# Down projection as seven quarter-size products, with weight sums added up in DRAM

## The chip, the cores and the metric

The kernel runs on one core of a Trainium2 chip. The metric is the device time of one execution, in microseconds (us). The kernel before takes 2771.59 us, the median of three runs (2770.87 to 2773.34).

## What is computed

One layer of a hybrid decoder over 512 tokens of width 2048, in float32. The change touches the last product, `w_down` (5632 x 2048):

```
u = rmsnorm(h, norm1);  p = u @ w_in                  # 2048 x 10272
y = [SSD scan | RG-LRU | mLSTM](p)                    # three mixers, 4096 channels
h = h + y @ w_out
g, v = split(rmsnorm(h, norm2) @ w_gate_up)           # 2 x 5632 columns
h = h + (silu(g) * v) @ w_down                        # 5632 -> 2048
out = rmsnorm(h, norm_f)
```

## The kernel before

Every large product is made in float32 precision from three passes: each operand is split into a high and a low part (ScalarE writes the rounded high part, VectorE subtracts it), and TensorE computes high x high, high x low and low x high into the same PSUM bank. `halves` (lines 739 to 745) does this for a weight tile of 128x1024, `split_into` for an activation tile of 128x512, `three` (line 747) issues the three matmuls.

The program has these stages. First the input projection and the mixers: the columns of `w_in` are cut into 80 units of 128, in the order of `UNITS`; `unit` loads two halves of 128x1024 (`load`, line 126, on SyncE's queue, three buffers named raw), splits them and issues 48 matmuls (lines 147 to 149). The first half of units 0, 1 and 2 is loaded ahead. Each group of six units feeds one group of the SSD mixer: `conv` (line 255) needs a small memset of its tile `cin` by GpSimd (line 258), the scan's PE work is lines 336 to 393, and GpSimd multiplies the results (`y`, line 399 and before, and `gsq`, all recorded under line 87); TensorE sums `gsq` in `ps_g` (line 408). Then the output projection (`w_out`), then `seven` (lines 904 to 969) for each of 11 blocks of 512 gate and up columns. `seven` already multiplies quarter matrices by a scheme of seven products in place of eight; its weight sums are made in SBUF by accumulating DMAs that GpSimd issues (`more`, line 930, tile `k`). Its results go to DRAM as `at` (line 925).

The down projection of before is a plain product: `down` (line 994) makes the output in four blocks of 512 columns over two ranges of the inner dimension (6 and 5 blocks of 512), each weight tile serving two rows of 128 x four token tiles, 24 matmuls a tile. Activations come back from `at` as `ae` and are split. `finish` computes the last norm for two token tiles at a time.

The source order of the program isn't the order on the engines: the kernel is built with a list scheduler (`schedule_with_timeline_sim=True`), which places every instruction on its engine's in-order program by its own estimate of when its operands are ready. SyncE (SP) issues nearly all DMAs, GpSimd (POOL) the accumulating ones. Each of the two has eight completion semaphores in turn, so a DMA of a queue waits for the landing of the one eight before it.

Of the kernel before, what the change touches and what calls it, by code (L numbers as in the profile page):

```python
# [27 lines left out]
FB = 4  # L28
NB = NF // FB
NG = 8  # L30
EPS = 1e-6
BIG = 3.0e38
GELU_C = 0.7978845608028654
# [33 lines left out]
def trunk(tc, A, out):  # L67
# [663 lines left out]
    def acc_bank():  # L731
        return ps_ac.tile([P, T], F32, name="ac", tag="ac")

    def raw_tile(src):
        r = wpool.tile([P, 2 * T], F32, name="raw", tag="raw", bufs=3)
        sync.dma_start(out=r, in_=src)
        return r

    def halves(r):
# [147 lines left out]

    at_d = [dram.tile([4, P, T], F32, name=f"at{j}") for j in range(NB)]  # L890
    with tc.tile_pool(name="gu", bufs=2, reuse_waits="tile") as gu:
        def wk(src, tag):
            r = gu.tile([P, 2 * T], F32, name=tag, tag=tag, bufs=4)
            sync.dma_start(out=r, in_=src)
            return r

        def acts_in(j, make):

            for t in range(4):
                e = gu.tile([P, T], F32, name="ae", tag="e", bufs=3)  # L900
                sync.dma_start(out=e, in_=at_d[j][t])
                acts[j, t] = split_into(e, make)

        def seven(j, done=None):
            def src(quad, n):
                return A["w_gu"][j, quad, n]

            def save(ps, name):
                o = [gu.tile([P, T], F32, name=name, tag=name) for _ in range(2)]
                for a in range(2):  # L910
                    actf(o[a], ps[a], AF.Copy)
                return o

            def swiglu(t, g, u):
# [24 lines left out]
            more(s, 1)  # L939
            if not done:  # L940
                block(2, b3, lambda n: raw_tile(src(2, n)))
            for a in range(2):
                tt(dve, r1[a], r1[a], b3[a], ALU.add)
            if last:
                acts_in(0, etile)
            block(5, b2, lambda n: s[n])
            r5 = save(b2, "r5")
            v = [wk(src(3, n), "k2") for n in range(4)]
            more(s, 3)
            if last:  # L950
                acts_in(1, xtile)
            block(6, b1, lambda n: s[n], first=False)
            r2 = save(b1, "r2")
            if last:
                acts_in(2, xtile)
# [10 lines left out]
            if last:  # L966
                for i in (3, 4, 5):
                    acts_in(i, vtile)
            for a in range(2):
                swiglu(a + 2, b1[a], r5[a])  # L970

        acts = {}
        seven(0, (b1, b3))
        for j in range(1, NB):
            seven(j)


    with tc.tile_pool(name="dn", bufs=1, reuse_waits="tile") as dn:
        h = []
        for t in range(4):  # L980
            ht = dn.tile([P, KD * P], F32, name=f"hf{t}")
            sync.dma_start(out=ht, in_=h_d[t])
            h.append(ht)
        nf = dn.tile([P, KD * P], F32, name="nf")
        sync.dma_start(out=nf, in_=A["norm_f"].to_broadcast([P, KD * P]))
        fstats = const.tile([P, 4, 4, 6], F32, name="fstats")

        def act_of(js):
            def f(k, t):
                f = k % 4  # L990
                return tuple(v[:, f * P:(f + 1) * P] for v in acts[js[0] + k // 4, t])
            return f

        def down(js, mb, ts):

            cols = slice(mb * T, (mb + 1) * T)
            ps = token_rows([A["w_down"][mb, n] for n in range(2 * js[0], 2 * js[-1] + 2)], act_of(js), ts)
            for t in ts:
                tt(dve, h[t][:, cols], h[t][:, cols], ps[t], ALU.add)
                if js[-1] == NB - 1:  # L1000
                    dve.bn_stats(out=fstats[:, t, mb], in_=h[t][:, cols])  # L1001
                    if mb < 3:
                        tt(pool, h[t][:, cols], h[t][:, cols], nf[:, cols], ALU.mult)

        def finish(ts):
            for t in ts:
                cols = slice(3 * T, 4 * T)
                fmv = const.tile([P, 1, 2], F32, name=f"fmv{t}")
                dve.bn_aggr(out=fmv[:, 0], in_=fstats[:, t].rearrange("p a b -> p (a b)"))
                r = rms(fmv, 1, f"rf{t}")  # L1010
                tt(pool, h[t][:, cols], h[t][:, cols], nf[:, cols], ALU.mult)
                half_row = KD * P // 2
                actf(h[t][:, 0:half_row], h[t][:, 0:half_row], AF.Copy, scale=r)
                sync.dma_start(out=out[t][:, 0:half_row], in_=h[t][:, 0:half_row])
                dve.tensor_scalar(out=h[t][:, half_row:], in0=h[t][:, half_row:], scalar1=r, scalar2=None, op0=ALU.mult)
                sync.dma_start(out=out[t][:, half_row:], in_=h[t][:, half_row:])

        js = range(0, 6)
        for mb in range(4):
            down(js, mb, range(4))  # L1020
        js = range(6, NB)
        for j, make in zip(js, (vtile, etile, xtile, xtile, vtile)):
            for t in range(4):
                e = dn.tile([P, T], F32, name="ae", bufs=3)
                sync.dma_start(out=e, in_=at_d[j][t])
                acts[j, t] = split_into(e, make)
        for mb in range(3):
            down(js, mb, range(4))
        for ts in ((0, 1), (2, 3)):
            down(js, 3, ts)  # L1030
            finish(ts)
# [35 lines left out]
def pack(x, norm1_w, w_in, ssd_conv_w, ssd_conv_b, ssd_dt_bias, ssd_a_log, ssd_d, ssd_norm_w,  # L1067
# [12 lines left out]
    a["w_down"] = moving(w_down[0])  # L1080
# [44 lines left out]
```

## Time and profile before

| | |
|---|---|
| median of the runs | 2771.59 us |
| the profiled execution | 2771.48 us |
| its span, first to last instruction | 2769.6 us |
| PE busy | 2733.8 us, 99% |
| DVE, ACT, POOL busy | 56%, 40%, 11% |
| DMA, mean | 154 GB/s; HBM read 384.43 MB, written 32.61 MB |

The profile has a page with the busy time of each engine and the chain of work that ended last, and the trace answers queries: a timeline of one engine, busy times in stretches (windows), groups of instructions by line. A stretch is given in us from the span's start. PE is TensorE, DVE is VectorE, ACT is ScalarE, POOL is GpSimd, SP is SyncE. MB is 10^6 bytes; a tile of 128x1024 float32 is 0.524 MB.

### The profile page before, as it was taken

How to read it: one execution, taken by the hardware profiler on the slowest of the kernel's cores; microseconds unless marked ns; L12 is line 12 of the kernel's file. 1: busy time of each engine (PE TensorE's matmuls, PEld its weight loads, DVE VectorE, ACT ScalarE, POOL GpSimd, SP SyncE). 2: the span in 40 equal slices, each digit the busy share in tenths (PEclk: the TensorE clock that was granted, in tenths of full speed). 3: DMA queues.
4: the chain of work that ended last, by engine and by line, in shares of the span. 5: the costliest groups of instructions: out<-in, count | busy, mean ns of one | idle time of the engine just before them, and what ended most of it. 6: DMA issues, size and time to landing. Idle time of an engine off the chain costs nothing.

```text
span 2769.6 us, 32286 instructions
## 1 busy us (share of the span) xinstructions
PE 2733.8 (99%) x12566; PEld 2236.9 (81%) x12566; DVE 1547.0 (56%) x2035; ACT 1104.8 (40%) x1319; POOL 314.5 (11%) x337
## 2 busy tenths in 40 slices
PE   8999999999999999999999999999999999999998
PEld 5888888888778877888878888888888878888886
DVE  8766666666677786324465555555555563233335
ACT  5433333333355565212244444444444452122113
POOL 2111111111011110000011112111111110000001
PEclk9999999999999999999999999999999999999999
DMA  4433333323233255544488898899888875234225
GB/s 170 136 107 106 111 107 102 97 98 120 89 125 131 100 179 175 168 153 138 143 223 212 205 202 197 206 203 200 198 202 204 216 196 212 94 112 133 99 92 182
DMA packets 139769, 425.46 MB, mean 154 GB/s; under 512 B 17052, under 2 KB 19132, under 8 KB 138976
## 3 DMA queue, kind: packets, MB, share of 16 engines
q1 hardware_dynamic: 114272, 331.11, 35.8%
q0 software_dynamic: 25344, 92.29, 18.4%
q8 instruction: 98, 1.61, 0.2%
q14 instruction: 55, 0.45, 0.1%
HBM read 384.43 MB, written 32.61 MB: 151 GB/s over the span
## 4 chain that ended last, share of the span: by engine, by line
PE 97%; DMA 1%; DVE 1%; ACT 0%; issue 0%; ACTq 0%; SPq 0%; DVEq 0%
PE ac L749 20%; PE ac L750 20%; PE ac L751 20%; PE mm L147 11%; PE mm L149 11%; PE mm L148 11%; PE ps_d L388 1%; PE tp L922 1%; DMA ae<-at 1%; PE ps_l L450 1%; DMA k<-in_w_gu 0%; PE ps_i L634 0%; PE ps_st L362 0%; PE ps_o L393 0%; PE ps_c L643 0%; DVE wlo L87 0%
## 5 line engine op out<-in xcount | busy, mean ns | idle before, releaser
L750 PE MATMUL ac<-wlo,vh 128*128 128x512 f32 x2192 | 857.8, 391 | 2.1 <-DVE wlo L87 1.9
L751 PE MATMUL ac<-whi,vl 128*128 128x512 f32 x2192 | 855.1, 391 | 0.0
L749 PE MATMUL ac<-whi,vh 128*128 128x512 f32 x2192 | 807.7, 391 | 6.6 <-ACT whi L93 6.6
L87 DVE TENSOR_TENSOR wlo<-raw,whi 128x1024 fp32r<-128x1024 f32 x370 | 457.8, 1237 | 608.7 <-ACT whi L93 599.0
L93 ACT ACTIVATE whi<-raw 128x1024 fp32r<-128x1024 f32 x370 | 391.5, 1058 | 942.8 <-PE ac L751 545.0
L147 PE MATMUL mm<-uh,whi 128*128 128x512 f32 x1280 | 507.4, 396 | 1.8 <-DVE og L87 1.0
L149 PE MATMUL mm<-uh,wlo 128*128 128x512 f32 x1280 | 504.6, 394 | 0.0
L148 PE MATMUL mm<-ul,whi 128*128 128x512 f32 x1280 | 504.1, 394 | 0.0
L749 PEld LDWEIGHTS ac<-whi,vh 128*128 128x128 f32 x2192 | 412.4, 188 | 95.4 <-ACT whi L93 7.7
L750 PEld LDWEIGHTS ac<-wlo,vh 128*128 128x128 f32 x2192 | 412.8, 188 | 90.3 <-DVE wlo L87 4.9
L87 DVE TENSOR_TENSOR wlo<-k,whi 128x1024 fp32r<-128x1024 f32 x260 | 318.2, 1225 | 295.4 <-ACT whi L93 294.0
L751 PEld LDWEIGHTS ac<-whi,vl 128*128 128x128 f32 x2192 | 412.6, 188 | 84.9 <-issue 0.2
L93 ACT ACTIVATE whi<-k 128x1024 fp32r<-128x1024 f32 x260 | 275.2, 1060 | 337.1 <-PE ac L751 306.9
L147 PEld LDWEIGHTS mm<-uh,whi 128*128 128x128 f32 x1280 | 240.5, 188 | 60.6 <-issue 6.9
L149 PEld LDWEIGHTS mm<-uh,wlo 128*128 128x128 f32 x1280 | 240.4, 188 | 53.8 <-issue 4.2
L148 PEld LDWEIGHTS mm<-ul,whi 128*128 128x128 f32 x1280 | 240.7, 188 | 50.8 <-issue 3.0
L930 POOL DMA_DIRECT2D k<-in_w_gu x176 | 152.5, 869 | 1015.2 <-DVE wlo L87 668.0
L749 PE MATMUL ac<-whi,uh 128*128 128x512 f32 x256 | 99.9, 390 | 0.0
L750 PE MATMUL ac<-wlo,uh 128*128 128x512 f32 x256 | 99.9, 390 | 0.0
L751 PE MATMUL ac<-whi,ul 128*128 128x512 f32 x256 | 99.0, 389 | 0.0
L90 DVE SCALAR_TENSOR_TENSOR cacc<-cin,half,cacc 128x512 f32<-128x512 f32 x96 | 81.2, 846 | 1.2
L87 POOL TENSOR_TENSOR hf<-hf,nf 128x512 f32<-128x512 f32 x16 | 25.1, 1594 | 485.9 <-DVE fstats L1001 485.9
(269 smaller groups left out, 1881.2 us busy)
## 6 DMA issues: line engine op xcount, KB each, us to landing
k<-in_w_gu POOLq DMA_DIRECT2D x176, 512.0 KB, 5.6
raw<-in_w_in SPq DMA_DIRECT2D x160, 512.0 KB, 3.7
raw<-in_w_down SPq DMA_DIRECT2D x98, 512.0 KB, 3.3
k<-in_w_gu SPq DMA_DIRECT2D x88, 512.0 KB, 4.1
raw<-in_w_out SPq DMA_DIRECT2D x64, 512.0 KB, 3.5
raw<-in_w_gu SPq DMA_DIRECT2D x48, 512.0 KB, 19.9
at<-e SPq DMA_DIRECT2D x44, 256.0 KB, 3.7
ae<-at SPq DMA_DIRECT2D x44, 256.0 KB, 4.1
```

The lines of the kernel that those rows point to most:

```text
L87: eng.tensor_tensor(out=o, in0=a, in1=b, op=op)
L90: dve.scalar_tensor_tensor(out=o, in0=a, scalar=s, in1=b, op0=op0, op1=op1)
L93: act.activation(out=o, in_=a, func=f, **kw)
L147: pe.matmul(ps, lhsT=wh, rhs=xh[:, cols], start=k == 0, stop=False)
L148: pe.matmul(ps, lhsT=wh, rhs=xl[:, cols], start=False, stop=False)
L149: pe.matmul(ps, lhsT=wl, rhs=xh[:, cols], start=False, stop=k == n - 1)
L388: pe.matmul(ps_d[i * 64:(i + 1) * 64, s], lhsT=xd[:, c, i * 64:(i + 1) * 64], rhs=es[i][:, s], start=True, stop=True)
L450: pe.matmul(ps, lhsT=lbd[:, k, :], rhs=xc, start=True, stop=True)
L749: pe.matmul(ps, lhsT=xh, rhs=wh, start=first, stop=False, skip_group_check=more)
L750: pe.matmul(ps, lhsT=xh, rhs=wl, start=False, stop=False, skip_group_check=more)
L751: pe.matmul(ps, lhsT=xl, rhs=wh, start=False, stop=last, skip_group_check=more)
L930: pool.dma_start(out=tiles[n], in_=src(quad, n), accum_op=ALU.add)
```

## The change

The down projection is cut into halves of tokens (a), of the inner dimension and of the columns (n), and made from seven products of quarters, in sequence, each over 22 slices of 128 of the inner dimension, two token tiles and two column blocks: 264 matmuls. Three of the seven use a quarter of `w_down` itself, and four use sums or differences of quarters, made beforehand in DRAM: `weight_sums` first copies a quarter slice to a DRAM tile `td` (plain DMA on SP), then adds another to it (accumulating DMA on POOL). In the source it is called at every third unit of the mixers.

```diff
     def project(kind, i):
-        return unit(index[kind, i], u)
+        n = index[kind, i]
+        if n % 3 == 2:
+            weight_sums(n // 3)
+        return unit(n, u)
...
+    td = [dram.tile([KH, P, KD * P // 2], F32, name=f"td{i}") for i in range(4)]
+
+    def weight_sums(step):
+        W = A["w_dn"]
+        if step < KH:
+            for o, q in ((0, 0), (2, 1), (1, 3), (3, 2)):
+                sync.dma_start(out=td[o][step], in_=W[q, step])
+        for lag, o, add in ((1, 0, W[1]), (1, 2, W[3]), (2, 1, td[0]), (3, 3, td[1])):
+            if 0 <= step - lag < KH:
+                pool.dma_start(out=td[o][step - lag], in_=add[step - lag], accum_op=ALU.add,
+                               max_dma_last_dim=KD * P // 2)
...
-                sync.dma_start(out=at_d[j][t], in_=e)
+                for i in range(2):
+                    sync.dma_start(out=at_d[2 * j + i, t // 2].rearrange("p (f t) -> p f t", f=2)[:, :, t % 2 * P:(t % 2 + 1) * P],
+                                   in_=e[:, 2 * i * P:2 * (i + 1) * P].rearrange("p (f t) -> p f t", f=2))
...
-        js = range(0, 6)
-        for mb in range(4):
-            down(js, mb, range(4))
...
+        def seventh(ps, xs, src, first=True):
+
+            for k in range(KH):
+                w = halves(raw_tile(src[k]))
+                for n in range(2):
+                    for t in range(2):
+                        three(ps[t][n], x_of(xs, k, t), w[n], first and k == 0, k == KH - 1, more=not first)
...
+        seventh(b2, dx, W[2])
+        x = operand(lambda k: x_in(0, 0, k))
+        into(h11, b2, ALU.add)
+        b1 = [[acc_bank(), acc_bank()], [tp_bank(), tp_bank()]]
+        seventh(b1, x, W[0])
+        x = operand(s5)
+        into(h11, b1, ALU.add, (0, 0))
+        b2 = four(acc_bank)
+        seventh(b2, x, td[0])
+        x = operand(s6)
+        h22 = quarter(1, 1)
+        into(h22, b2, ALU.subtract)
+        seventh(b1, x, td[1], False)
+        x = operand(s3)
+        h12 = quarter(0, 1)
+        into(h12, b1, ALU.subtract)
+        seventh(b2, x, W[3], False)
+        x = operand(s7)
+        into(h12, b2, ALU.subtract, (0, 1))
+        seventh(b1, x, td[2], False)
...
```

The seventh product (with `td[3]`) runs over one column block after the other, so that the first can be finished under the second. `x_in` reads a slice of `at` into a tile `ax`, s5, s6, s3 and s7 form sums of activation quarters in the tiles `ch` (one or two 128x512 operations of DVE a slice), `operand` splits them, `into` adds a product to the rows of `h` (tiles `hq`).

The scheduler's order moves with it. On SP, the start of the program after the last input tile, before (raw is the weight tile of a unit, cs_d and csb are the decay sums of the SSD mixer):

```order
L217 DMA xq_196<-in_xT 128x1024 x2
L445 DMA lbd<-in_lru_bd 128x256
L126 DMA raw<-in_w_in 128x1024 x11
L298 DMA cs_d<-cs 32x512
L299 DMA cend_d<-cend 32x4
L377 DMA csb<-cs_d 128x512 x2
```

and now, the first rows and, behind the "...", the last of the copies (td_271, td_272, td_273 and td_274 are `td[0]` to `td[3]`):

```order
L218 DMA xq_196<-in_xT 128x1024 x2
L288 DMA td_271<-in_w_dn 16x8192
L288 DMA td_273<-in_w_dn 16x8192
L288 DMA td_272<-in_w_dn 16x8192
L288 DMA td_274<-in_w_dn 16x8192
...
L288 DMA td_272<-in_w_dn 16x8192
L288 DMA td_274<-in_w_dn 16x8192
L127 DMA raw<-in_w_in 128x1024 x3
L394 DMA csb<-cs_d 128x512 x4
L326 DMA cend_b<-cend_d 128x128
```

All 88 copies stand ahead of the seventh raw tile; only three raw tiles lie among them (behind 5, 35 and 37 copies).

On POOL, the rows of the first SSD group, before:

```order
L231 TENSOR_SCALAR uh<-xq_196,vecs 128x512 x2
L258 MEMSET cin 128x3 x4
L87 TENSOR_TENSOR y<-y,ecs 128x384
L87 TENSOR_TENSOR y<-y,zs 128x512
```

and now the last accumulating DMAs, with the semaphores that they wait for (DMASW0 to DMASW7 are POOL's eight):

```order
L291 DMA td_274<-td_272 512x256 [waits DMASW2_49]
L291 DMA td_274<-td_272 512x256 [waits DMASW3_49]
L88 TENSOR_TENSOR y<-y,zs 128x512 [waits DVE_49,Pool_49]
L291 DMA td_274<-td_272 512x256 [waits DMASW4_49]
L88 TENSOR_TENSOR gsq<-gsq 128x512 [waits PE_49,Activation_49]
L291 DMA td_274<-td_272 512x256 [waits DMASW5_49]
L291 DMA td_274<-td_272 512x256 [waits DMAHW0_49,DMASW6_49]
L291 DMA td_274<-td_272 512x256 [waits DMAHW4_49,DMASW7_49]
L262 MEMSET cin 128x3 [waits DVE_49,Activation_49] x2
```

Between the input tiles and `gsq` POOL now has 85 of the 88 accumulating DMAs; the other three stand right behind it. Each is cut into 512 pieces of 256 elements.

On PE, the first sum of `gsq`, before (lines 147 to 149 are the matmuls of the units):

```order
L149 MATMUL mm<-uh,wlo 128x512
L147 MATMUL mm<-uh,whi 128x512
L408 MATMUL ps_g<-gsq,ones 32x128 x4
L148 MATMUL mm<-ul,whi 128x512
```

and now:

```order
L149 MATMUL mm<-ul,whi 128x512
L150 MATMUL mm<-uh,wlo 128x512
L425 MATMUL ps_g<-gsq,ones 32x128 x4
L148 MATMUL mm<-uh,whi 128x512
```

Ahead of `ps_g` stood 442 matmuls of units, now 288 (six whole units); the work of the first SSD group stands ahead of it in both.

## Rows read from the trace of the kernel before

**Rows 1.** The page: busy time by engine; the chain that ended last.

```profile
PE 2733.8 (99%) x12566; PEld 2236.9 (81%) x12566; DVE 1547.0 (56%) x2035; ACT 1104.8 (40%) x1319; POOL 314.5 (11%) x337
...
PE 97%; DMA 1%; DVE 1%; ACT 0%; issue 0%; ACTq 0%; SPq 0%; DVEq 0%
```

**Rows 2.** Windows: length, busy of PE, PEld, DVE, ACT, POOL; clock, DMA share, GB/s.

```profile
100.00:1000.00 900.00, 898.18 (x4392) 735.29 (x4391) 595.87 (x963) 369.05 (x481) 111.59 (x115) 1.00 0.33 108
1500.00:2300.00 800.00, 797.65 (x3576) 657.62 (x3575) 446.70 (x445) 387.46 (x445) 135.04 (x156) 1.00 0.87 202
2300.00:2700.00 400.00, 400.00 (x1768) 331.33 (x1767) 125.37 (x126) 90.97 (x95) 12.05 (x8) 1.00 0.37 123
```

**Rows 3.** Timeline of PE, start and length in us, near the first ps_g.

```profile
123.23 0.39 PE L147 MATMUL mm<-uh,whi 128*128 128x512 f32 x1
...
127.99 0.39 PE L147 MATMUL mm<-uh,whi 128*128 128x512 f32 x1
...
132.39 0.43 PE L408 MATMUL ps_g<-gsq,ones 128*32 128x128 f32 x8
```

**Rows 4.** Timeline of SP's DMA queue, the first 70 us.

```profile
10.87 1.63 SPq L217 DMA_DIRECT2D xq<-in_xT  x2
13.46 0.33 SPq L445 DMA_DIRECT2D lbd<-in_lru_bd  x1
14.81 54.18 SPq L126 DMA_DIRECT2D raw<-in_w_in  x11
```

**Rows 5.** Windows as in rows 2: plain loads alone, accumulating DMAs alone.

```profile
10.00:20.00 10.00, 9.71 (x38) 4.38 (x42) 9.53 (x17) 8.29 (x10) 8.47 (x5) 1.00 1.03 406
1590.00:1620.00 30.00, 30.00 (x134) 24.86 (x133) 15.23 (x14) 14.45 (x16) 9.52 (x11) 1.00 1.05 190
```

**Rows 6.** The page: DMA queues, packets, MB, share of 16 engines' span.

```profile
q1 hardware_dynamic: 114272, 331.11, 35.8%
q0 software_dynamic: 25344, 92.29, 18.4%
```

**Rows 7.** Timeline of POOL, its products in the first SSD group.

```profile
107.16 1.86 POOL L87 TENSOR_TENSOR y<-y,ecs 128x384 f32<-128x384 f32 x1 [34.02 <-DVE ecs L87]
...
127.10 3.06 POOL L87 TENSOR_TENSOR gsq<-gsq 128x512 f32<-128x512 f32 x1 [1.78 <-ACT gsq L93]
```

**Rows 8.** Groups by line and shape, 2300 to 2757 us: busy, mean ns, idle before.

```profile
L87 DVE TENSOR_TENSOR wlo<-raw,whi 128x1024 fp32r<-128x1024 f32 x92 | 115.0, 1249 | 280.9 <-ACT whi L93 280.9
L93 ACT ACTIVATE whi<-raw 128x1024 fp32r<-128x1024 f32 x92 | 97.6, 1061 | 325.2 <-PE ac L751 299.7 <-DVE hf L87 17.5 <-DMA raw<-in_w_down 6.3
L87 DVE TENSOR_TENSOR hf<-hf,ac 128x512 f32<-128x512 f32 x32 | 21.7, 684 | 11.3 <-PE ac L751 11.3
L87 DVE TENSOR_TENSOR vl<-ae,vh 128x512 fp32r<-128x512 f32 x20 | 13.7, 692 | 7.4 <-PE ac L750 4.3 <-ACT vh L93 2.7 <-PE ac L751 0.4
L93 ACT ACTIVATE vh<-ae 128x512 fp32r<-128x512 f32 x20 | 12.6, 632 | 14.4 <-DMA ae<-at 5.5 <-PE ac L751 4.7 <-PE ac L750 3.8
```

**Rows 9.** Timeline of the end: last matmul, last statistics, last store's issue.

```profile
2756.31 0.39 PE L751 MATMUL ac<-whi,vl 128*128 128x512 f32 x1
2757.34 1.28 DVE L1001 BATCH_NORM_STATS2 fstats<-hf 128x6 f32<-128x512 f32 x2
...
2763.76 1.14 SPq L1014 DMA_DIRECT2D out_dram<-hf  x1
```

**Rows 10.** DMA issues by line: count, KB each, median us to landing.

```profile
raw<-in_w_down SPq DMA_DIRECT2D x98, 512.0 KB, 3.3
k<-in_w_gu SPq DMA_DIRECT2D x88, 512.0 KB, 4.1
raw<-in_w_out SPq DMA_DIRECT2D x64, 512.0 KB, 3.5
raw<-in_w_gu SPq DMA_DIRECT2D x48, 512.0 KB, 19.9
at<-e SPq DMA_DIRECT2D x44, 256.0 KB, 3.7
```

More of the change, by code (lines that the diff above doesn't have):

```diff
@@ L732, in acc_bank, with tp_bank, raw_tile @@
         return ps_ac.tile([P, T], F32, name="ac", tag="ac")
-    def raw_tile(src):
+    def tp_bank():
+        return ps_tp.tile([P, T], F32, name="tp", tag="tp")
+    def raw_tile(src, two=False):
         r = wpool.tile([P, 2 * T], F32, name="raw", tag="raw", bufs=3)
-        sync.dma_start(out=r, in_=src)
+        sync.dma_start(out=r.rearrange("p (k f) -> p k f", k=2) if two else r, in_=src)
         return r
@@ L884, in trunk @@
     stt(rs2, rs, -1.0, rsh, ALU.mult, ALU.mult)
-    at_d = [dram.tile([4, P, T], F32, name=f"at{j}") for j in range(NB)]
+    at_d = {(k, a): dram.tile([P, T], F32, name=f"at{k}{a}") for k in range(KH) for a in range(2)}
     with tc.tile_pool(name="gu", bufs=2, reuse_waits="tile") as gu:
@@ L895, in wk, with slot, first_operand @@
             return r
-        def acts_in(j, make):
-            for t in range(4):
+        ring = [etile] * 8 + [xtile] * 17 + [vtile] * 32
+        turn = [0]
+        def slot(dt, name):
+            turn[0] += 1
+            return ring[(turn[0] - 1) % len(ring)](dt, name)
+        def first_operand(ks):
+            for k in ks:
                 e = gu.tile([P, T], F32, name="ae", tag="e", bufs=3)
-                sync.dma_start(out=e, in_=at_d[j][t])
-                acts[j, t] = split_into(e, make)
+                sync.dma_start(out=e, in_=at_d[k, 0])
+                dx.append(split_into(e, slot))
         def seven(j, done=None):
@@ L944, in seven @@
             if last:
-                acts_in(0, etile)
+                first_operand(range(0, 4))
             block(5, b2, lambda n: s[n])
@@ L950, in seven @@
             if last:
-                acts_in(1, xtile)
+                first_operand(range(4, 8))
             block(6, b1, lambda n: s[n], first=False)
@@ L965, in seven @@
             block(4, b1, lambda n: s[n], first=False)
-            if last:
-                for i in (3, 4, 5):
-                    acts_in(i, vtile)
             for a in range(2):
                 swiglu(a + 2, b1[a], r5[a])
-        acts = {}
+        dx = []
         seven(0, (b1, b3))
@@ L975, in trunk @@
             seven(j)
+    HF = KD * P // 2
     with tc.tile_pool(name="dn", bufs=1, reuse_waits="tile") as dn:
[L979 to L985, printed above, removed]
-        fstats = const.tile([P, 4, 4, 6], F32, name="fstats")
[L988 to L991, printed above, removed]
-            return f
@@ L994, in down @@
[L994 to L1016, printed above, removed]
@@ new lines, in trunk, with quarter, x_in, operand @@
+        chain = []
+        def quarter(a, n):
+            hq = dn.tile([P, 2, HF], F32, name="hq", tag="hq", bufs=3)
+            for t in range(2):
+                sync.dma_start(out=hq[:, t], in_=h_d[2 * a + t][:, n * HF:(n + 1) * HF])
+            return hq
+        def x_in(kh, a, k):
+            e = dn.tile([P, T], F32, name="ax", tag="ax", bufs=2)
+            sync.dma_start(out=e, in_=at_d[k + KH // 2 * (1 - kh), a])
+            return e
+        def operand(make):
+            return [split_into(make(k), slot) for k in range(KH // 2)]
@@ new lines, in s5, with s6, s3 @@
+        def s5(k):
+            c = dn.tile([P, T], F32, name="ch", tag="ch", bufs=KH // 2)
+            sync.dma_start(out=c, in_=at_d[k, 1])
+            tt(dve, c, c, x_in(0, 1, k), ALU.subtract)
+            chain.append(c)
+            return c
+        def s6(k):
+            stt(chain[k], chain[k], -1.0, x_in(0, 0, k), ALU.mult, ALU.subtract)
+            return chain[k]
+        def s3(k):
+            stt(chain[k], chain[k], -1.0, x_in(1, 0, k), ALU.mult, ALU.subtract)
+            return chain[k]
@@ new lines, in s7, with x_of @@
+        def s7(k):
+            e, f = x_in(0, 0, k), x_in(0, 1, k)
+            tt(dve, f, e, f, ALU.subtract)
+            return f
+        def x_of(xs, k, t):
+            o = k % 2 * 2 * P + t * P
+            return tuple(v[:, o:o + P] for v in xs[k // 2])
+        def seventh(ps, xs, src, first=True):
+            for k in range(KH):
+                w = halves(raw_tile(src[k]))
+                for n in range(2):
+                    for t in range(2):
+                        three(ps[t][n], x_of(xs, k, t), w[n], first and k == 0, k == KH - 1, more=not first)
@@ new lines, in four, with into, rsqrt_of @@
+        def four(make):
+            return [[make() for _ in range(2)] for _ in range(2)]
+        def into(hq, ps, op, done=None, ns=(0, 1)):
+            for t in range(2):
+                for n in ns:
+                    o = hq[:, t, n * T:(n + 1) * T]
+                    tt(dve, o, o, ps[t][n], op)
+                    if done:
+                        dve.bn_stats(out=fstats[:, 2 * done[0] + t, 2 * done[1] + n], in_=o)
+        def rsqrt_of(t):
+            fmv = const.tile([P, 1, 2], F32, name=f"fmv{t}")
+            dve.bn_aggr(out=fmv[:, 0], in_=fstats[:, t].rearrange("p a b -> p (a b)"))
+            return rms(fmv, 1, f"rf{t}")
@@ new lines, in trunk @@
+        into(h12, b2, ALU.subtract, (0, 1))
+        seventh(b1, x, td[2], False)
+        nf = []
+        for n in range(4):
+            nf.append(dn.tile([P, T], F32, name="nf", tag="ch", bufs=KH // 2))
+            sync.dma_start(out=nf[n], in_=A["norm_f"][:, n * T:(n + 1) * T].to_broadcast([P, T]))
+        for t in range(2):
+            r = rsqrt_of(t)
+            for m, hq in ((0, h11), (1, h12)):
+                for n in range(2):
+                    times_nf(hq, t, n, m)
+                put_out(0, t, m, r, hq)
@@ new lines, in trunk @@
+        x = operand(lambda k: x_in(1, 1, k))
+        into(h22, b1, ALU.subtract, (1, 1))
+        h21 = quarter(1, 0)
+        into(h21, b1, ALU.add)
+        for t in range(2):
+            for n in range(2):
+                times_nf(h22, t, n, 1)
+        b2 = four(acc_bank)
+        for n in range(2):
+            for k in range(KH // 2):
+                w = halves(raw_tile(td[3][2 * k:2 * k + 2, :, n * T:(n + 1) * T].rearrange("k p f -> p k f"), two=True))
+                for i in range(2):
+                    for t in range(2):
+                        three(b2[t][n], x_of(x, 2 * k + i, t), w[i], k + i == 0, k == KH // 2 - 1 and i == 1)
+            into(h21, b2, ALU.add, (1, 0), (n,))
+            if n == 0:
+                for t in range(2):
+                    times_nf(h21, t, 0, 0)
@@ L1032, in trunk @@
+        for t in range(2):
+            r = rsqrt_of(2 + t)
+            o = h21[:, t, T:]
+            stt(o, o, r, nf[1], ALU.mult, ALU.mult)
+            sync.dma_start(out=out[2 + t][:, T:HF], in_=o)
+            o = h21[:, t, 0:T]
+            dve.tensor_scalar(out=o, in0=o, scalar1=r, scalar2=None, op0=ALU.mult)
+            sync.dma_start(out=out[2 + t][:, 0:T], in_=o)
+            put_out(1, t, 1, r, h22)
     xpool_cm.__exit__(None, None, None)
```

26 lines of the change are left out of this document (13 added, 13 removed).

## The prediction
> **What bounds the kernel now.** I read the page first: PE is busy for 99% of the span and the chain that ended last is PE for 97% of it [rows 1]. So time is saved by taking matmuls away, and lost wherever PE is made to stand. Then the windows by stage [rows 2]: the DMA engines are a third busy in the mixers (108 GB/s), 0.87 in the gate/up stage and 0.37 in the down projection; there PE has no gap in 400 us. This is the room in which the change wants to put its copies. Then the start of the program, since the scheduler's order puts the new DMAs there and not spread over the mixers: what SP and POOL do in the first 130 us [rows 4, 7], what DMAs can move at most [rows 5, 6], and how far PE has come by then [rows 3].
>
> PE starts a matmul of 512 columns every 0.2267 us: two starts of line 147, 21 matmuls apart, lie 127.99 - 123.23 = 4.76 us apart [rows 3]. Sums are made against the profiled execution's 2771.48 us, which is the median of the runs within 0.1 us.
>
> **Matmuls removed.** Before, the down projection has 44 slices x 4 column blocks x 4 token tiles x 3 = 2112 matmuls; after, 7 x 264 = 1848. 264 x 0.2267 = 59.8 us, all on PE's path: **-59.8 us**.
>
> **The down stage's other work.** The seven products last 1848 x 0.2267 = 419 us. In them DVE has 154 weight tiles x 1.249, 66 operand splits x 0.692, 44 sums of activation quarters (priced as a split, 0.69), 32 additions and 16 statistics x 0.684 [rows 8]: 192 + 46 + 30 + 22 + 11 = 301 us, 72%. ACT has 154 x 1.061 + 66 x 0.632 = 205 us, 49%. DMA has 154 x 0.524 + 88 x 0.262 + 8 x 0.524 MB = 108 MB, 258 GB/s, against 406 seen in a stretch of plain loads [rows 5]. All fits beside PE. What gets tight is the pace: a weight tile now serves 12 matmuls, 2.72 us, where it served 24. A raw buffer is taken for 3.3 (landing, rows 10) + 1.06 + 1.25 = 5.6 us, and there are three: one tile per 1.9 us. The gate/up stage already runs at 12 matmuls a tile, with busier DMA, and its PE is idle for 2.35 us in 800 [rows 2]. But here bursts of DVE come at the seams of the products, and SP holds back weight loads behind the stores of the first half's output and the reload of `hq`. I take **+15 us**; the ends are 0 (the gate/up row) and 40 (six seams of some 6 us, one such seam being an `into` of four additions and four statistics, 8 x 0.684 = 5.5 us).
>
> The stores to `at` become two for each one, 44 more; SP's issue takes 0.33 us [rows 4] and one landed in 3.7 us [rows 10], nothing on PE's path follows closely, so I cost them at nothing; if a read of `at` catches up with them it is some us once. The tail is as before: last matmul, additions, statistics, norm, scaling, store [rows 9], 15 us to the end of the execution, no term.
>
> **The start.** Here is the large term. Two queues carry it.
>
> On SP, the seventh raw tile, the one that unit 3 needs, stands behind 88 copies. Before, it was issued within the 11 raw loads that start at 14.81 us [rows 4].
>
> On POOL, `gsq` of the first SSD group stands behind 85 accumulating DMAs. Number 85 is issued only when number 77 has landed. PE's `ps_g` needs `gsq`, and PE's program behind it is all the rest of the kernel; ACT and DVE also queue there. Before, POOL multiplied at 107 to 130 us, waiting only for DVE and ACT [rows 7]. So PE passes `ps_g` not before 88 copies, 77 accumulating DMAs and the loads of the first six units are through the 16 DMA engines, whichever order they take.
>
> How far has PE come by then? Before, `ps_g` ran at 132.39 us, with 442 unit matmuls ahead of it; now it has 288 ahead. So PE's work ahead of the new `ps_g` is what the old program had done at 132.4 - 154 x 0.2267 = 97.5 us. What `ps_g` is late beyond 97.5 us, the end is late too, since nothing behind has idle PE to give back [rows 1].
>
> The bytes: copies 88 x 0.524 = 46.1 MB; accumulations 77 x 0.524 = 40.4 MB; loads (8 input tiles, 12 raw, 11 csb of 0.262, about 1 MB of small ones) 14.4 MB.
>
> The prices: plain loads from DRAM to SBUF ran at 406 GB/s with the engines' share at 1.03, so full [rows 5]; the loads take 14.4 / 0.406 = 35 us. Accumulating DMAs into SBUF, alone for 30 us, ran at 190 GB/s, also full (1.05) [rows 5]; over the whole span the two queues give 331.11 MB in 35.8% and 92.29 MB in 18.4% of 2769.6 us, 334 and 181 GB/s [rows 6]. No row shows a copy or an accumulation from DRAM to DRAM. A copy: at best like a plain load, 46.1 / 0.406 = 114 us; at worst like an accumulation, which also moves two streams of bytes for one of result, 46.1 / 0.190 = 243 us. I take the dear end, as each byte passes DRAM twice. An accumulation: at best the 190 row, 40.4 / 0.190 = 213 us; at worst half that rate, 425 us, for its target now lies in DRAM and its pieces are of 1 KB where the row's were rows of 4 KB. I take the row itself, which is the same operation.
>
> The Trainium skill ("DMA: Bandwidth & Descriptors", Latency and other measured facts) gives about 207 to 214 GB/s for copies between DRAM tensors; by 214 the copies would take an estimated 215 us, and the whole forecast would be 28 us lower. No row here shows such a copy.
>
> Sum: 2 us until the first DMA + 35 + 243 + 213 = 493, and 5 us for the last issues and the 3.06 us of `gsq` [rows 7]: `ps_g` at 498 us. Late by 498 - 97.5 = **+400 us**. Bounds: 2 + 35 + 114 + 213 + 5 = 369, late by 272; and 2 + 35 + 243 + 425 + 5 = 710, late by 613. A gain here is excluded: PE cannot have `gsq` earlier than DVE and ACT give it.
>
> The mixers behind it and the gate/up stage stay as they are, PE-bound.
>
> **Total:** 2771.5 + 400 - 59.8 + 15 = **3127 us**.
>
> **Rivals.**
>
> *Only reading costs.* Copies run at the plain load's 406 GB/s and accumulations at 190, the low bound above: 2771.5 + 272 - 59.8 + 15 = 2998 us. For it: the 190 row is just under half of the 406 row, as if two reads were all that an accumulation costs. Against: both rows write to SBUF. The Trainium skill ("Collectives: The Full Stack", The bandwidth ceiling) has this rule: a reducing transfer is half as fast as a copy because it reads two sources through the same ring, not for the addition. By that rule, the trace agrees for SBUF targets (190 / 406 = 0.47); no run shows DRAM targets.
>
> *It hides: the other side.* The engines find time for the 92 MB in the two thirds that the mixers leave free [rows 2], and the units' loads get through between the copies. Then nothing is late and the kernel is **faster**: 2771.5 - 59.8 + 15 = 2727 us. It needs raw loads and `gsq` to pass the new DMAs, that is, a start that is at most 45 us late decides between a gain and a loss. For it: the source spreads the calls over 22 x 3 units. Against: the order on SP and POOL, and 77 accumulations of 0.524 MB that even at 190 GB/s end long after 97.5 us.
>
> *Only SP's queue holds.* POOL's accumulations keep up with the copies and PE waits for raw tiles alone. Unit 3 needs the copies and about 20 us of loads: 2 + 20 + 243 = 265 us, where the old program stood at three units (97.5 less three units of 48 matmuls and 7 us of SSD work, 58 us): late by 207, total 2934 us. Against: while copies run, accumulations share their engines.
>
> *Pieces cost, not bytes.* A packet of POOL's queue took 0.184 x 2769.6 x 16 / 25344 = 0.32 us [rows 6], nearly all of them 4 KB. If a piece of 1 KB takes as long, 77 x 512 x 0.32 / 16 = 788 us instead of 213: `ps_g` at 1073 us, total 3702 us. Against: the plain queue's packets, 2.9 KB each on average, took 0.358 x 2769.6 x 16 / 114272 = 0.14 us, and the input tiles' stretch at 406 GB/s shows engines that are full by bytes.
>
> **Chances.** Forecast (both queues hold, prices between the bounds) 0.63; only reading 0.20; pieces 0.08; only SP 0.05; hidden 0.04. About 0.2% (5 us) is what a measurement of this kernel tells from no change. Faster comes only from the hidden case: 0.04; same 0.01, its slow edge; slower 0.95. The range runs from the low bound with no stall in the down stage, 2771.5 + 272 - 59.8 = 2983, taken as 2980, to the high one with 40 us of stalls, 2771.5 + 613 - 59.8 + 40 = 3365. Outside lie the pieces, SP alone and the hidden case, 0.17 together.
>
> **What would show it.** Right: the first ten or so slices of the page show PE mostly idle and DMA at 9; `ps_g` (line 425) starts first near 500 us; the waits list POOL's first `y` and `gsq` and ACT behind them for hundreds of us; the down stage is 419 us of PE plus some 15, and the span after `ps_g` is the old one less 60. The copies' rate can be read from the landing of SP's line 288, the accumulations' from POOL's line 291. Wrong: if raw tiles land during the copies, or if POOL's `y` runs near 107 us, the large term falls; if DRAM targets cost much more than SBUF ones, `ps_g` comes beyond 700 us.

## The result, and the profile after

The changed kernel takes **3066.2 us** (median of 4 runs, 3061.12 to 3074.43) against 2772.08 us before, measured beside it (4 runs, 2770.87 to 2773.34). The ratio is **1.106, 95% interval 1.105 to 1.108**. The forecast was 3127 with a range of 2980 to 3365. The profiled execution is the slowest of the four, 3074.43 us, with a span of 3072.7.

The page of the changed kernel: busy time by engine, three rows of the 40 slices (each 77 us), the DMA queues, the chain that ended last.

```profile
PE 2702.1 (88%) x12302; PEld 2197.2 (72%) x12302; DVE 1660.1 (54%) x2168; ACT 1182.0 (38%) x1410; POOL 400.1 (13%) x423
...
PE   4221169999999999999999999999999999988998
...
PEclk7665589999999999999999999999999999999999
DMA  9999993333323233256443698888889887887765
...
q1 hardware_dynamic: 154784, 421.04, 40.7%
q0 software_dynamic: 71808, 138.43, 26.7%
...
PE 72%; DMA 13%; issue 7%; DVE 5%; ACT 2%; POOL 1%; SPq 0%; another core or an unknown queue 0%; DVEq 0%; POOLq 0%; ACTq 0%
```

PE was busy for 99% and owned 97% of the chain [rows 1]; now it is 88% and 72%. The slices say where: in the first six (I had said ten or so) PE is mostly idle and DMA is at 9, and from the seventh on the mixers look as before, DMA at 3. q0 grew by 46.1 MB, the 88 accumulations; q1 by 90 MB, of which 46.1 are the copies.

The start as two windows (columns as in rows 2), and PE's timeline at the first `ps_g`:

```profile
0.00:200.00 200.00, 56.40 (x237) 35.80 (x238) 54.42 (x87) 31.93 (x36) 32.44 (x38) 0.65 1.02 309
200.00:400.00 200.00, 47.23 (x204) 37.04 (x203) 31.72 (x70) 18.24 (x27) 68.25 (x70) 0.60 1.20 199
```

```profile
417.81 0.65 PE L425 MATMUL ps_g<-gsq,ones 128*32 128x128 f32 x8 [21.36 <-POOL gsq L88]
419.81 0.79 PE L148 MATMUL mm<-uh,whi 128*128 128x512 f32 x1 [1.34 <-ACT whi L94]
```

In 400 us PE works for 104, and the DMA engines are full throughout. `ps_g` runs at 417.8 us, where PE's work would have let it run at 97.5: it is **320.3 us late**. The releaser is the one forecast, `gsq` on POOL [rows 7].

SP's queue shows the first reason. These are its rows up to the seventh raw tile (start, length, what, count):

```profile
14.65 4.99 SPq L288 DMA_DIRECT2D td<-in_w_dn  x5
19.76 0.50 SPq L127 DMA_DIRECT2D raw<-in_w_in  x1
20.30 52.91 SPq L288 DMA_DIRECT2D td<-in_w_dn  x30
...
80.58 56.20 SPq L288 DMA_DIRECT2D td<-in_w_dn  x29
...
170.98 10.96 SPq L288 DMA_DIRECT2D td<-in_w_dn  x8
183.22 3.58 SPq L127 DMA_DIRECT2D raw<-in_w_in  x3
```

All copies are issued by 182 us. The raw tile that unit 3 needs leaves at 183.22, where it was one of the 11 loads from 14.81 on [rows 4].

POOL shows the second. Its timeline, first in a stretch where nothing but accumulations stands, then at the end of them:

```profile
352.69 1.01 POOL L291 DMA_DIRECT2D td<-td  x1 [1.28 <-DMA td<-td]
355.32 1.01 POOL L291 DMA_DIRECT2D td<-td  x1 [1.62 <-DMA td<-td]
358.00 1.01 POOL L291 DMA_DIRECT2D td<-td  x1 [1.67 <-DMA td<-td]
360.67 1.01 POOL L291 DMA_DIRECT2D td<-td  x1 [1.65 <-DMA td<-td]
...
415.44 1.03 POOL L291 DMA_DIRECT2D td<-td  x1 [2.23 <-DMA td<-td]
416.11 1.65 POOL L88 TENSOR_TENSOR gsq<-gsq 128x512 f32<-128x512 f32 x1
418.56 1.01 POOL L291 DMA_DIRECT2D td<-td  x1 [0.80 <-DMA td<-td]
```

An accumulation of 0.524 MB goes out every 2.66 us, when an earlier one has landed: 197 GB/s. `gsq` stands behind the 85th and runs 0.7 us after its issue starts.

The waits of the first 450 us (total, times, longest) name both queues and those who stand behind them:

```profile
POOL td L291 <- DMA td<-in_w_dn: 223.1, 47, 28.6
...
ACT whi L94 <- DMA raw<-in_w_in: 139.4, 7, 86.4
...
ACT ecs L94 <- POOL y L88: 120.2, 2, 115.6
```

**The books.** The last `ps_s` of the SSD part runs at 935.7 us against 608.8 before (+326.9), the first transpose of the gate/up stage at 1802.0 against 1472.2 (+329.8), the end at +303.1. So `ps_g` is late by 320, some 10 us are lost behind it, and from there to the end the kernel wins 26.7 us instead of 59.8: the down stage stalls for 33. In its 420 us from 2630 to 3050 PE is busy for 394.60.

### The profile page after: what moved, and what is told of

Read it like the earlier page. It is cut to its first block, busy times and chain, and to the rows that moved or that the text cites. A ratio compares the mean times of both kernels' runs of the same rounds, so it can differ in the third digit from the quotient of the medians.

```text
span 3072.7 us, 32607 instructions
## 1 busy us (share of the span) xinstructions
PE 2702.1 (88%) x12302; PEld 2197.2 (72%) x12302; DVE 1660.1 (54%) x2168; ACT 1182.0 (38%) x1410; POOL 400.1 (13%) x423
## 3 DMA queue, kind: packets, MB, share of 16 engines
q0 software_dynamic: 71808, 138.43, 26.7%
## 4 chain that ended last, share of the span: by engine, by line
PE 72%; DMA 13%; issue 7%; DVE 5%; ACT 2%; POOL 1%; SPq 0%; another core or an unknown queue 0%; DVEq 0%; POOLq 0%; ACTq 0%
PE ac L770 14%; PE ac L769 14%; PE ac L771 14%; PE mm L148 8%; PE mm L150 8%; PE mm L149 8%; DMA ax<-at 3%; DMA td<-in_w_dn 3%; DMA td<-td 2%; DVE wlo L88 2%; DMA k<-in_w_gu 1%; POOL td L291 1%; DVE vl L88 1%; ACT whi L94 1%; PE tp L951 1%
## 5 line engine op out<-in xcount | busy, mean ns | idle before, releaser
L88 DVE TENSOR_TENSOR wlo<-raw,whi 128x1024 fp32r<-128x1024 f32 x426 | 529.9, 1246 | 580.7 <-ACT whi L94 570.8
L770 PE MATMUL ac<-wlo,vh 128*128 128x512 f32 x1972 | 777.3, 394 | 20.6 <-DVE wlo L88 20.2
L94 ACT ACTIVATE whi<-raw 128x1024 fp32r<-128x1024 f32 x426 | 448.7, 1057 | 887.9 <-PE ac L771 302.6
L771 PE MATMUL ac<-whi,vl 128*128 128x512 f32 x1972 | 772.7, 392 | 0.0
L769 PE MATMUL ac<-whi,vh 128*128 128x512 f32 x1972 | 692.5, 392 | 12.2 <-ACT whi L94 12.2
L770 PEld LDWEIGHTS ac<-wlo,vh 128*128 128x128 f32 x1972 | 372.0, 189 | 110.2 <-DVE wlo L88 33.6
L769 PEld LDWEIGHTS ac<-whi,vh 128*128 128x128 f32 x1972 | 370.8, 188 | 94.5 <-ACT whi L94 15.7
L771 PEld LDWEIGHTS ac<-whi,vl 128*128 128x128 f32 x1972 | 372.3, 189 | 75.8 <-issue 0.2
L410 PE MATMUL ps_o<-cT,hs 128*128 128x128 f32 x96 | 19.0, 284 | 108.1 <-DVE hs L88 108.1
L91 DVE SCALAR_TENSOR_TENSOR csb<-csb,tok,cmat 128x128 f32<-128x128 f32 x128 | 44.5, 411 | 111.2 <-ACT ecs L94 110.9
```

The source lines that it names most:

```text
L88: eng.tensor_tensor(out=o, in0=a, in1=b, op=op)
L91: dve.scalar_tensor_tensor(out=o, in0=a, scalar=s, in1=b, op0=op0, op1=op1)
L94: act.activation(out=o, in_=a, func=f, **kw)
L769: pe.matmul(ps, lhsT=xh, rhs=wh, start=first, stop=False, skip_group_check=more)
L770: pe.matmul(ps, lhsT=xh, rhs=wl, start=False, stop=False, skip_group_check=more)
L771: pe.matmul(ps, lhsT=xl, rhs=wh, start=False, stop=last, skip_group_check=more)
```

## The experiments

Theory: the copies hold SP's queue and the accumulations hold POOL's, both in order, and PE waits for whichever ends last; the down stage loses some tens of us besides. Rivals: one queue alone, the bytes wherever they are moved, the 1 KB pieces.

### e1: both kinds of transfer kept in their place in the program

```diff
-                sync.dma_start(out=td[o][step], in_=W[q, step])
+                tc.keep_in_program_order(sync.dma_start(out=td[o][step], in_=W[q, step]))
...
-                pool.dma_start(out=td[o][step - lag], in_=add[step - lag], accum_op=ALU.add,
-                               max_dma_last_dim=KD * P // 2)
+                tc.keep_in_program_order(pool.dma_start(
+                    out=td[o][step - lag], in_=add[step - lag], accum_op=ALU.add,
+                    max_dma_last_dim=KD * P // 2))
```

> Every copy and every accumulating DMA is pinned behind the instruction that the source has before it on its queue, so that they are spread over the mixers; nothing else changes. If the loss is that PE waits for the two queues at the start (ps_g 320 us late), it goes away here: ps_g near 100 to 135 us, and 2771.5 - 59.8 + some 35 to 45 us of stalls in the down stage = 2747 to 2757 us. If the loss is contention between 92 MB of new traffic and the units' loads, wherever it runs, it stays in part: 5 us for each of 22 steps would give 2850 us or more.

Measured: **2758.49 us, ratio 0.995 (0.993 to 0.997)**, 1.5 us above the range of the first theory and far from the second. The bytes are the same, and the loss at the start is gone. Windows of e1 in the SSD part and behind it:

```profile
100.00:600.00 500.00, 500.00 (x2513) 411.93 (x2510) 321.78 (x506) 179.06 (x239) 111.33 (x115) 1.00 0.82 218
600.00:1000.00 400.00, 388.56 (x1824) 313.91 (x1823) 263.86 (x443) 184.29 (x235) 68.57 (x79) 0.99 0.65 177
```

With 0.82 of the DMA engines busy PE has no gap in the 500 us of the first window. What cost 300 us was the order, not the traffic. Between 600 and 1000 something is lost; that is for e6 to e10.

### e2: only the accumulations kept in place

The second half of the edit of e1; the copies go to SP's front as in the change.

> Only the accumulating DMAs are pinned in program order; the copies stay at the start of SP's queue as in the change. SP's queue then holds PE alone. By the theory of two queues the copies run alone, 46.1 MB at 300 to 406 GB/s, 114 to 155 us, and the seventh raw tile is 80 to 120 us late: 2825 to 2870 us. If POOL's queue makes all of the loss, 2750 us; if SP's queue makes all of it, 3066 us.

Measured: 2862.2 us (one run). The last `ps_s` runs at 726.3, against 610.0 in e1 and 935.7 in the change: **SP's queue alone costs 116 us there, POOL's a further 209.** (The other order, with the copies in place and the accumulations at the front, was not run.) The copies now have the DMA engines nearly to themselves (a raw tile goes between them, and two accumulations beside the second stretch), and SP's timeline gives their price:

```profile
19.81 44.54 SPq L288 DMA_DIRECT2D td<-in_w_dn  x30
...
71.41 47.48 SPq L288 DMA_DIRECT2D td<-in_w_dn  x29
...
160.68 3.02 SPq L127 DMA_DIRECT2D raw<-in_w_in  x3
```

A copy takes 44.54 / 30 = 1.48 to 47.48 / 29 = 1.64 us, 353 to 320 GB/s of result. From 118 to 160 us, where PE stands and almost nothing but copies runs, the engines move 321 GB/s at a share of 1.03.

### e3: no sums at all

```diff
-            weight_sums(n // 3)
+            pass
...
-        seventh(b2, x, td[0])
+        seventh(b2, x, W[0])
```

and likewise for the other three products with `td`.

> The copies and the accumulating DMAs are left out, and the four products that use sums of weight quarters read a plain quarter of w_down in their place. This prices the seven products alone: 2771.5 - 59.8 + 35 to 45 us of stalls in the down stage = 2747 to 2757 us. If the time behind ps_g in the change was longer because of the td traffic or because of the late start, the stalls are gone here: 2712 to 2720 us.

Measured: **2742.15 us, ratio 0.989 (0.988 to 0.991)**, between the two ranges and in neither. 2770.94 - 59.8 = 2711.1, so some **31 us are lost in the down stage** though nothing is copied; the stalls don't come of the late start. Window and waits of that stage:

```profile
2300.00:2720.00 420.00, 398.73 (x1712) 321.03 (x1712) 275.18 (x305) 193.19 (x216) 28.25 (x14) 0.99 0.73 248
```

```profile
ACT whi L94 <- DMA raw<-in_w_dn: 76.1, 51, 5.8
...
ACT vh L94 <- DVE ax L88: 36.6, 10, 5.0
DVE ax L88 <- DMA ax<-at: 30.5, 11, 3.9
```

PE is idle for 21.3 us of the 420. The waits suggest `ax`, which has two buffers: SP loads the next only when one is free, and VectorE and ScalarE queue behind it.

### e4: pieces of 4 KB instead of 1 KB

```diff
-                               max_dma_last_dim=KD * P // 2)
+                               max_dma_last_dim=4 * (KD * P // 2))
```

> The accumulating DMAs are cut into rows of 4 KB in place of pieces of 1 KB; the order of the instructions stays. If bytes cost, the last 40 accumulations start 2.6 to 2.8 us apart as in the change, and the time stays at 3050 to 3080 us. If each piece has a price of its own, they come faster: at 2.0 us each ps_g is some 50 us earlier, 3015 us.

Measured: 3034.41 us (one run), in neither of the ranges; `ps_g` at 381.8 instead of 417.8. From POOL's timeline:

```profile
327.72 0.81 POOL L291 DMA_DIRECT2D td<-td  x1 [1.68 <-DMA td<-td]
330.20 0.81 POOL L291 DMA_DIRECT2D td<-td  x1 [1.67 <-DMA td<-td]
332.69 0.81 POOL L291 DMA_DIRECT2D td<-td  x1 [1.68 <-DMA td<-td]
```

2.49 us apart, not 2.66: a quarter of the pieces saves 6% of the time between two accumulations. The bytes set most of it. But `ps_g` comes 36 us earlier, and 77 x 0.17 us are 13 of them, so the pieces of 1 KB cost more than this spacing shows. From 300 to 350 us accumulations run alone in both; e4's window, against 186 GB/s at a share of 1.21 in the change:

```profile
300.00:350.00 50.00, 2.72 (x6) 1.61 (x7) 6.07 (x16) 6.62 (x9) 18.42 (x23) 0.50 1.06 208
```

And by the time the last copy is issued, 28 accumulations are out in e4 (at 206 us) and 14 in the change (at 182 us). Why the small pieces hold them back beside the copies was not traced.

### e5: eight `ax` tiles instead of two (on e3)

```diff
-            e = dn.tile([P, T], F32, name="ax", tag="ax", bufs=2)
+            e = etile(F32, "ax") if turn[0] >= 14 + KH else dn.tile([P, T], F32, name="ax", tag="ax", bufs=2)
```

and the ring goes on without the eight `etile` slots once the first operand has had them.

> Left out, as in e3: the weight sums (the products take plain weight quarters, so two launches' worth of time is not at stake, only the sums' copies and accumulations). Against e3 one thing changes: from the second operand of the down stage on, the tiles ax, into which the act quarters are loaded back, rotate through the eight tiles of the pool extra instead of two; the ring that holds the operands' halves has 49 tiles then instead of 57. e3 took 2742.15 us, and its PE stood still for 21 us between 2300 and 2720. Theory (the stage's stalls are ax loads that SP issues only when one of two buffers is free, with VectorE and ScalarE queued in order behind them): PE still for under 10 us there, 2720 to 2732 us, the ax waits of DVE (30.5 us over 11) gone. Rival A (the stage is held by the pace at which ScalarE and VectorE split weight halves and operand halves, whatever waits are named): 2738 to 2745. Rival B (the shorter ring lets fewer halves be made ahead): 2745 to 2760.

Measured: **2744.75 us, ratio 0.990 (0.988 to 0.991)**, the same as e3: rival A's number, and a miss for my theory. Window and waits of e5:

```profile
2300.00:2720.00 420.00, 398.62 (x1697) 321.25 (x1696) 276.54 (x304) 190.66 (x215) 28.03 (x14) 0.98 0.74 247
```

```profile
ACT whi L94 <- DMA raw<-in_w_dn: 91.2, 49, 6.8
...
DVE ax L88 <- DMA ax<-at: 10.9, 8, 2.8
```

The wait that I had blamed fell from 30.5 to 10.9 us, the wait for weights rose from 76.1 to 91.2, and PE stands exactly as long. A wait that is named often need not be the one that counts. The shorter ring (rival B) changed along with the buffers, so that a gain from the one and a loss from the other cancel is not excluded.

### e8: one operand for all products (on e3)

```diff
-        x = operand(s5)
...
-        x = operand(lambda k: x_in(1, 1, k))
```

with the three between them gone too.

> Left out, beside the weight sums as in e3: the five later first operands of the down stage. The act quarters of the second product are used again by all that follow, so nothing is loaded into ax, subtracted or split between the products; the seven products read, split and multiply their weights as in e3. Question: what keeps PE idle for 21 us between 2300 and 2720 in e3, if not the number of ax buffers (e5). Theory 1 (forming the operands: their loads, subtractions and splits stand in the in-order queues of SyncE, VectorE and ScalarE ahead of weight halves): PE idle falls under 8 us, 2718 to 2730 us. Theory 2 (the weights alone: 22 tiles per product at a pace of 2.72 us each through three raw buffers, with the DMA engines 0.93 busy at the stage's start): 2736 to 2744.

Measured: **2714.85 us, ratio 0.979 (0.978 to 0.981)**. The window that answers to e3's:

```profile
2270.00:2690.00 420.00, 415.48 (x1828) 341.43 (x1828) 230.80 (x219) 174.92 (x174) 28.60 (x14) 1.00 0.65 215
```

PE is idle for 4.5 us instead of 21.3, and 27 of the 31 us are gone (below the lower end that I gave). The idle time tells 17 of them; the matmuls tell all: 1828 in these 420 us against 1712 in e3's, and 116 x 0.2267 = 26 us. Weights at 2.72 us a tile through three buffers keep up; **forming the operands is what stalls the stage**, a first theory that was right about the work and, as far as e5 tells, wrong about the buffers. Which of its parts decides (loads in SP's order, the DMA bytes, subtractions and splits on VectorE) was not separated.

### e6 and e7: the loss between 600 and 1100

e6 is e1 with the pieces of e4. e7 is e6 with the eight transfers of a step dealt out over the three units that it spans:

```diff
-        if n % 3 == 2:
-            weight_sums(n // 3)
+        if n >= 2:
+            weight_sums((n - 2) // 3, (n - 2) % 3)
```

> e1 (copies and accumulations both kept in their place in the program, 2758.49 us) with accumulations in rows of 4 KB instead of 1 KB. e1 lost 16 us against e3 between 620 and 1100, where GpSimd's accumulations waited for copies to land (41 us over 6 waits) and weight tiles came late. Theory 1 (the DMA engines are full there for stretches of some 17 us, and e4 showed an accumulation 2.49 instead of 2.66 us apart): a little of it comes back, 2752 to 2757. Theory 2 (it is the order in GpSimd's and SyncE's queues alone, a burst of four copies ahead of the weights, no matter how wide the rows): 2757 to 2761.

> e6 with the eight transfers of a step dealt out over the three units that a step spans (two copies and one accumulation, two copies and one, two accumulations) instead of all eight at every third unit. Theory 1 (the loss between 620 and 1100 comes of bursts: four copies of 1.5 us and four accumulations of 2.5 us stand ahead of the weight tiles of the next unit): most of the 16 us come back, 2743 to 2750. Theory 2 (the amount of traffic costs it, however it is dealt out): within 3 us of e6. Rival (GpSimd now stops at more places, since each accumulation waits for a copy with fewer units between): 2760 to 2775.

Measured: e6 **2775.68 us, ratio 1.001 (1.0005 to 1.002)**, 17 us slower than e1 with cheaper transfers (15 when each is set against the kernel before measured beside it), outside both theories' numbers. e7 **2764.28 us, ratio 0.997 (0.996 to 0.998)**: 11 better than e6 and no better than e1. It misses both theories and lies in the range of the rival, whose mechanism (GpSimd stops at more places) was not tested. The longest piece of e6's chain of waits near 660 says what happened there, and POOL's timeline what came before:

```profile
659.08 15.68 DMA w<-in_ml_w
```

```profile
640.01 1.49 POOL L88 TENSOR_TENSOR gsq<-gsq 128x512 f32<-128x512 f32 x1 [0.75 <-ACT gsq L94]
641.44 0.13 POOL L262 MEMSET mx<- 128x3 f32 x2
641.51 1.65 POOL L291 DMA_DIRECT2D td<-in_w_dn  x2
642.58 2.27 POOL L291 DMA_DIRECT2D td<-td  x2
...
643.73 2.91 POOL L291 DMA_DIRECT2D td<-in_w_dn  x2
```

The last products of the SSD part hold POOL until 640. Then the accumulations that had gathered behind them go out in a bunch, and the mLSTM's small table `w`, wanted just then, takes 15.7 us. VectorE waits for it, with the next weight half queued behind, and PE stands for 8.2 us between 660 and 680, where e1 had no gap. That accounts for half of the loss; the rest was not traced. `w` took 14.3 us in e7 too, where VectorE waited for it as well, and 2.8 in the change and 2.9 in e9 (below), which have no accumulations there. But e1 has the same bunch (from 642.71) and nothing waits for its `w`, issued 2 us earlier, at 657.0. So that traffic in this stretch makes the small loads late is shown; that wider pieces made e6 slower than e1, and not a difference of a few us in when the two meet, is not.

### e9 and e10: no sums in that stretch

The 176 transfers in one list, three at each of units 2 to 47 (the SSD part), none in the LRU and mLSTM units, the last 38 one by one ahead of weight tiles of the output projection: from its first tile in e9, from its 17th in e10.

```diff
-        if n % 3 == 2:
-            weight_sums(n // 3)
+        if 2 <= n < 48:
+            weight_sums(3)
...
+            rows_of[0] += 1
+            if rows_of[0] > 16:
+                weight_sums(1)
             w = halves(raw_tile(src))
```

> The 176 transfers of the sums, in rows of 4 KB and each in its place in the program, dealt out otherwise: three for each of the units 2 to 47 (the SSD part), none for the LRU and mLSTM units, and the last 38 one by one ahead of the weight tiles of the output projection, where GpSimd has nothing to do and the DMA engines were 0.42 busy in e3. Theory (what e1 and e6 lost between 600 and 1100 came of accumulations that stood in GpSimd's queue ahead of that stretch's own small steps, in a bunch of seven or eight behind the last y*zs at 640): that loss goes, 2742 to 2749 us, the best kernel that forms the sums. Rival A (the output projection has three weight buffers, and each 2.5 us accumulation makes a weight tile late): PE idle 10 to 20 us between 1090 and 1290, 2753 to 2765. Rival B (three transfers per unit are more than the SSD part can carry, 0.9 of the DMA engines' time and more): PE idle between 100 and 600, over 2765.

> e9 with the last 38 transfers one by one ahead of the 17th to the 54th weight tile of the output projection instead of the 1st to the 38th. e9 equalled e3 between 600 and 1000 and lost some 6 us between 1090 and 1160, where the DMA engines were 1.05 busy against 0.67 in e3: the y and x tiles that open the projection came late. Theory (the collision at the projection's opening is all that is left before it): PE busy as in e3 from 1090 to 1160, 2744 to 2750 us. Rival (the projection has no room for the accumulations at any place, or they collide with the h and hx tiles at the block ends): another 5 to 10 us lost between 1160 and 1500, 2750 to 2757.

Measured: e9 **2751.8 us, ratio 0.992 (0.991 to 0.994)**, between the theory's range and rival A's; e10 **2748.54 us, ratio 0.992 (0.990 to 0.993)**, in the theory's range. Windows of e9, then of e10:

```profile
600.00:1000.00 400.00, 398.17 (x1890) 323.51 (x1889) 275.53 (x459) 190.55 (x243) 40.66 (x52) 1.00 0.33 111
1000.00:1090.00 90.00, 85.95 (x356) 67.92 (x355) 65.86 (x85) 56.55 (x68) 13.98 (x9) 0.96 0.62 202
1090.00:1160.00 70.00, 64.32 (x273) 51.63 (x271) 20.80 (x24) 13.97 (x16) 9.94 (x12) 0.98 1.05 292
```

```profile
100.00:600.00 500.00, 498.81 (x2503) 410.62 (x2504) 325.14 (x512) 178.70 (x238) 117.53 (x123) 1.00 0.82 231
...
1090.00:1160.00 70.00, 67.75 (x294) 54.57 (x294) 29.48 (x35) 19.04 (x24) 7.08 (x9) 1.00 0.99 287
1160.00:1500.00 340.00, 333.41 (x1492) 274.97 (x1491) 159.83 (x197) 102.20 (x117) 26.23 (x31) 0.99 0.72 212
```

In e9 the stretch from 600 to 1000 is whole again: 398.17 of 400 against e1's 388.56 and e3's 397.95. The loss moved to the opening of the projection, where the engines are full at 1.05 and PE loses 5.7 us; so the theory and rival A each came true in part. In e10's trace later placement wins over half of that back, and nothing is lost after 1160 (333.41 against e3's 333.31). In time e9 and e10 are level against the kernel before, 0.992 both, so this gain is seen in the traces only. e10 forms all four sums and is **0.8% faster than the kernel before, 10% faster than the change**; 6 us separate it from e3, which forms none.

## Why the prediction was right, step by step

The forecast was 61 us too high, or 53 against the profiled 3074.43, and that it came so near is in part luck: the copies were priced 106 us too dear and the accumulations 8, and 34 us at the start, 10 behind it and 18 in the down stage were missing, which takes 62 of it back.

**Matmuls removed, -59.8 us: held.** e8, which keeps the products and drops the operand work, takes 2714.85 us where 2773.37 - 59.8 = 2713.6.

**The start, +400 us: the mechanism held, one term was mis-sized.** `ps_g` was late by 320.3. Both queues hold it, as e2 and e1 show by giving back one and then both. The prices:

- *Copies, 243 us at 190 GB/s: the step that failed.* I took the dear end, "as each byte passes DRAM twice". e2's rows give 1.48 to 1.64 us for one, 88 of them 131 to 144 us. A plain load of that size takes 0.524 / 0.406 = 1.29 us [rows 5], so a copy into DRAM costs 15 to 27% more than a load into SBUF, and not twice as much. The Trainium skill ("DMA: Bandwidth & Descriptors", Latency and other measured facts) gives its 207 to 214 GB/s for tiles of 128 rows of 16 KB in tensors whose rows lie far apart. The copies here are contiguous, 512 KB each, and ran at 320 to 353, so that figure doesn't carry over to them.
- *Accumulations, 213 us at 190 GB/s: held.* 77 x 2.66 = 205. A target in DRAM costs no more than one in SBUF (197 against 190 GB/s), and pieces of 1 KB some 6% more than 4 KB while accumulations run alone. The rule in the Trainium skill ("Collectives: The Full Stack", The bandwidth ceiling), given there for the steps of a ring collective, that a reducing transfer is half as fast as a copy because it reads two sources, comes near what e2 and the change show, 197 against 320 to 353 GB/s, or 0.56 to 0.62.
- With measured prices the sum is 2 + 35 + 137 + 205 + 5 = 384, and `ps_g` came at 417.8. Some 34 us were not in my list. Most of them go with the pieces of 1 KB: in e4 the same sum is 2 + 35 + 137 + 77 x 2.49 + 5 = 371, and `ps_g` came at 381.8, 11 us later. A further reason may be that I let all loads run at 406 GB/s, where between 200 and 400 us the engines moved 199 in all, at a share of 1.20; that was not tested.

**The work behind stays as it is: nearly.** Some 10 us are lost between `ps_g` and the gate/up stage, which I had at nothing. Two of them are the first eight unit matmuls behind `ps_g`, which take 3.9 us at the lower clock (419.81 to 423.69) where eight take 1.8; the rest stays open, and the 97.5 us from which the 320 is counted is an estimate too.

**The down stage, +15 us: mis-sized, inside its ends of 0 and 40.** It lost 33, and 31 in e3. I argued from the gate/up stage, which runs at the same 12 matmuls a tile with 2.35 us idle [rows 2], and thought of the seams. The stalls come of forming the next product's operand beside the running one (e8): DVE was priced by its mean, 72% busy, and a mean says little where three engines work in order, each behind the other.

**The rivals.** *Only reading costs* (2998) had the accumulations right and the copies too cheap; the result lies halfway between it and the forecast. *Only SP's queue* (2934) falls by e2: that case, built, takes 2862, and POOL's queue adds 204. *Pieces* (3702) falls by the spacing: it asks for 512 x 0.32 / 16 = 10.2 us an accumulation, and 2.66 were seen; by e4 the small pieces cost some 36 us in all. *It hides* (2727) is not what this kernel does, but it comes near what e1 and e10 do: it asked that raw loads and `gsq` pass the new transfers, and keeping the program's order brings that about. Set beside e3, its time was too low by the stalls of the down stage.

## What to carry to other kernels

A transfer that waits for nothing may be moved to the front of an in-order queue, and everything that queue carries then waits for it; look at the order as scheduled, not at the place of the call in the source. Before adding background traffic, ask of each queue what small urgent things stand behind it, and place the traffic where those are rare: against e3, the same bytes cost 324 us at the front, 16 to 31 spread over all the mixers (e1, e6) and 6 away from the stretch that has such things. Where a stage's engines hand work to each other in order, test a suspected wait by removing the work, since adding buffers may only rename the wait.

## What the runs showed of the hardware that I had not expected

- Copies between DRAM tensors ran at 320 to 353 GB/s of result (e2), an accumulation into DRAM at 197 (210 in pieces of 4 KB, e4), no slower than the 190 into SBUF [rows 5].
- The DMA engines' share is no measure of bytes: accumulations alone read 1.21 at 186 GB/s in pieces of 1 KB and 1.06 at 208 in pieces of 4 KB (300 to 350 us, the change and e4), plain loads 1.03 at 406 [rows 5].
- From 300 to 350 us, where PE did nothing at all, its granted clock was 0.50, the lower of its two levels (1.2 of 2.4 GHz), and the first unit matmul behind `ps_g` took 0.79 us against 0.39 [rows 3]. So a long stall costs a little more than its length, here the 2 us named above. The window of the changed kernel:

```profile
300.00:350.00 50.00, 0.00 (x0) 0.00 (x0) 0.00 (x0) 0.00 (x0) 18.36 (x19) 0.50 1.21 186
```
